# Eight conditioning columns moved out of attention's up projection, and loads of x put between the out projection's weights

## The chip, the cores and the metric

The kernel runs on one core of one Trainium2 chip. The metric is the device time of one execution in microseconds (us). TensorE (PE in the profile) does the matmuls, VectorE (DVE) and ScalarE (ACT) the elementwise work, and SyncE's queue (SP) issues nearly all loads and stores.

## The reference, cut to what matters

One block of a diffusion transformer over 1024 tokens of width 1024. A conditioning vector c gives six column vectors, and the block uses them in this order:

```python
ada = silu(c) @ w_ada + b_ada
sh1, sc1, g1, sh2, sc2, g2 = split(ada, 6)
...
mixed = (g_hy * y_hy + g_att * y_att) @ w_out
x = x + g1 * rmsnorm(mixed, g_mix_post)
hf = rmsnorm(x, g_ffn_pre) * (1 + sc2) + sh2
f = (silu(hf @ w_gate) * (hf @ w_up)) @ w_down
x = x + g2 * rmsnorm(f, g_ffn_post)
```

Here y_att is attention's output times its half of the up weights (attention's up projection), w_out is the out projection, and w_gate, w_up and w_down (width 2816) are the feed-forward part. sc2 is first needed after the out projection, g2 only at the end of the down projection.

## The kernel before, in words

Everything is kept transposed, features on the 128 partitions. Each matmul operand is split into a rounded part ("hi", cast by ACT) and a rest ("lo", subtracted on DVE), and every product is three matmuls: hi by hi, hi by lo, lo by hi. A weight tile is therefore loaded to wraw, cast to whi by ACT (L126) and its wlo is made on DVE (L77 is the helper for all two-tensor operations), before the PE can use it. wraw, whi and wlo have two buffers each.

**A conditioning column** is one column of `cols` (128 numbers). ada_tile (L142 to L146) loads 128 rows of w_ada, 512 KB, into a tile wada_t and multiplies and sums it against silu(c), spread over all partitions, in one DVE instruction on 128x1024 (L145). Columns 0 to 15 (sh1, sc1) are made by matmul at the start, 16 to 31 (g1, sh2) by ada_tile beside attention. The list `jobs` holds columns 32 to 47: sc2 is 32 to 39, g2 is 40 to 47. Tiles wada_t have two buffers here (NWB).

**Attention's up projection** (att_up, L972, called from L983) goes over eight tiles m of the output. Each tile has one weight load of 256 KB (wup), four loads of 256 KB of stored gates (g), 24 matmuls (L134), four sigmoids on ACT, two casts, and on DVE one wlo and eight operations on 128x512: per half the products mix by gate and ps by gate, their sum, and the rest ml. After every two tiles two columns of `jobs` are made (L987 to L989), eight in all: sc2.

**The out projection** (L1128) goes over two halves n of the tokens, two halves z of the output and four pieces q of the weights (wout). A piece is loaded as two halves of 256 KB into one wraw (wide_raw, L1028) and is used for 24 matmuls (rows, L1043). Pieces are counted here from 0 to 15. Two of them are loaded ahead, and wo.next() loads the piece two further on and splits the next. At the head of each half n the eight tiles of x of that half (xh, 256 KB each, L1131) are loaded for the residual. In the half n = 0 one column is made after each piece: columns 40 to 47, g2. A generator `between` turns the result, adds x, makes the second norm and writes x2d; it runs in steps between later matmuls.

**Gate and up** (L1384) goes over products of 12 matmuls each (L1181): for 24 head products and then seven or five products per weight column j (a seven-product scheme for 2x2 blocks). Each product's weights are cast and split (need) one product ahead (LA = 1): the first eight matmuls use whi, the last four wlo. Tiles "xc" have 16 buffers: first x, later results. Tiles "c11" have three, used in the head and at the end. **The down projection** (L1509) is a similar scheme over stored hidden tiles; down_gain needs g2 there (mcol columns 32 to 39).

**What sets the order**: nothing is timed by hand beyond the order of the text. The framework under the kernel orders each engine's instructions by its own estimate of when their inputs and buffers are free, with earlier text first among those that are ready; then each engine and each DMA queue works its list strictly in order. So a load can stand far from where the text has it.

Of the kernel before, what the change touches and what calls it, by code (L numbers as in the profile page):

```python
# [9 lines left out]
F32 = mybir.dt.float32  # L10
F32R = mybir.dt.float32r
I32 = mybir.dt.int32
AF = mybir.ActivationFunctionType
ALU = mybir.AluOpType
# [3 lines left out]
P = 128  # L18

L, D, C, DFF = 1024, 1024, 256, 2816  # L20
KD = D // P
# [8 lines left out]
NWB = 2  # L30
# [28 lines left out]
V_BADA, V_GMPRE, V_GMPOST, V_GFPRE, V_GFPOST = 0, 48, 56, 64, 72  # L59
# [4 lines left out]
def block_kernel(tc, xT, ctxT, cvec, cT, wada1, wada, vecs, lamv, dbias, zT, fw1, fw2, fv, fw3, decay, mfs, mis, rope,  # L64
                 win, wup, wout, wgate, wupf, wdown, outT):
    nc = tc.nc
    V, A, G, T = nc.vector, nc.scalar, nc.gpsimd, nc.tensor
# [8 lines left out]
    def tt(out, a, b, op, eng=None):  # L76
        (eng or V).tensor_tensor(out=out, in0=a, in1=b, op=op)  # L77
# [7 lines left out]
    def act(out, in_, func, bias=0.0, scale=1.0, **k):  # L85
        A.activation(out=out, in_=in_, func=func, bias=bias, scale=scale, **k)
# [14 lines left out]
    cp = root.enter_context(pool("consts", side="left"))  # L101
# [7 lines left out]
    vec = cp.tile([P, NV], F32, name="vec")  # L109
    nc.sync.dma_start(out=vec, in_=vecs)  # L110
    cols = cp.tile([P, 64], F32, name="cols")
    lamc = cp.tile([P, 4], F32, name="lamc")
    mcol = cp.tile([P, 48], F32, name="mcol")
# [28 lines left out]
    def ada_tile(dstcol, sbc, j, tag_pool, nb=NWA):  # L142
        w = tag_pool.tile([P, D], F32, tag="wada", bufs=nb, name="wada_t")
        nc.sync.dma_start(out=w, in_=wada[j - 16])
        V.tensor_tensor_reduce(out=w, in0=w, in1=sbc, scale=1.0, scalar=vec[:, V_BADA + j:V_BADA + j + 1],  # L145
                               op0=ALU.mult, op1=ALU.add, accum_out=dstcol)  # L146
# [510 lines left out]
    for i in range(2):  # L657
        V.tensor_tensor_reduce(out=lamt[:, i * 128:i * 128 + 64], in0=lamt[:, i * 128:i * 128 + 64],
                               in1=lamt[:, i * 128 + 64:i * 128 + 128], scale=1.0, scalar=0.0,
                               op0=ALU.mult, op1=ALU.add, accum_out=lamc[:, i:i + 1])  # L660
# [190 lines left out]
    left = {}  # L851
# [103 lines left out]
    for n in range(2):  # L955
        dg = mp.tile([P, 512], F32, tag="dg", bufs=2, name="dg")
        sl = slice(n * 512, (n + 1) * 512)
# [25 lines left out]
    for m in range(0, 8, 2):  # L983
        ups = [att_up(m), att_up(m + 1)]
        for i in UPO if m == 6 else (0, 0, 1, 1):
            next(ups[i])
        for j in jobs[:2]:  # L987
            ada_tile(cols[:, j:j + 1], sc3, j, left["gp"], NWB)
        jobs = jobs[2:]  # L989
    yst.close()  # L990
    ms_.close()

# [10 lines left out]
    def xc(name):  # L1003
        return rt.tile([P, 512], F32, tag="xc", bufs=16, name=name)
# [89 lines left out]
    def between(n):  # L1094

        sl = slice(n * 512, (n + 1) * 512)
        scale_rows(n, rows_rstd(ssq[:, n], D))
        yield
        acc2 = mp.tile([P, 512], F32, tag="accq", bufs=2, name="accq")

        for k in range(KD):
            z, kq = divmod(k, 4)
            pt = bank2()
            for b in range(4):
                T.transpose(out=pt[:, b * P:(b + 1) * P], in_=om[n, b, z][:, kq * P:(kq + 1) * P], identity=ident)
            stt(xh[n][k], pt, mcol[:, 16 + k:17 + k], xh[n][k], ALU.mult, ALU.add)
            sq_acc(acc2, xh[n][k], k == 0, mp)
            nc.sync.dma_start(out=x2d[:, k, sl], in_=xh[n][k])
        yield
        dg = rstd_dg(pacc, acc2, 512, D, mp, "tr", 2)  # L1110
        yield
        bc = diag_bc(pacc, dg, 512, "tr", 2)
        for k in range(KD):
            stt(xh[n][k], xh[n][k], mcol[:, 24 + k:25 + k], bc, ALU.mult, ALU.mult)
            sh = cols[:, 24 + k:25 + k]
            if n == 0:
                X0[k] = split_tile(rt, "hfa", 16)
                act(X0[k][0], xh[n][k], AF.Identity, bias=sh)
                stt(X0[k][1], xh[n][k], sh, f(X0[k][0]), ALU.add, ALU.subtract)
            else:  # L1120
                act(xh[n][k], xh[n][k], AF.Identity, bias=sh)
        yield
# [4 lines left out]
    wo.split()  # L1127
    for n in range(2):  # L1128
        sl = slice(n * 512, (n + 1) * 512)
        for k in range(KD):  # L1130
            nc.sync.dma_start(out=xh[n][k], in_=xT[k][:, sl])  # L1131
        for z in range(2):
            acc = [bank() for b in range(4)]
            for q in range(4):
                w = wo.next()
                rows(acc, w, [(mixh[k][:, sl], mixl[k][:, sl]) for k in (2 * q, 2 * q + 1)], q == 0, q == 3)
                if n == 1 and 4 * z + q in S0:
                    next(mid)
                if n == 0:
                    for j in jobs[:1]:  # L1140
                        ada_tile(cols[:, j:j + 1], sc3, j, mp, NWB)
                    jobs = jobs[1:]
            for b in range(4):
                sq = mp.tile([P, 512], F32, tag="sqt", bufs=SQB, name="sqt")
                act(sq, acc[b], AF.Square, accum_out=ssq[:, n, b, z:z + 1])
                om[n, b, z] = mp.tile([P, 512], F32, tag="om", bufs=8, name="om")
                A.copy(out=om[n, b, z], in_=acc[b])
        if n == 0:
            mid = between(0)
            tt(mcol[:, 16:24], vec[:, V_GMPOST:V_GMPOST + 8], cols[:, 16:24], ALU.mult)  # L1150
            stt(mcol[:, 24:32], cols[:, 32:40], 1.0, vec[:, V_GFPRE:V_GFPRE + 8], ALU.add, ALU.mult)
        else:
            tt(mcol[:, 32:40], vec[:, V_GFPOST:V_GFPOST + 8], cols[:, 40:48], ALU.mult)
    mx.close()


# [67 lines left out]
    def c11_tile():  # L1224
        return gp.tile([P, 512], F32, tag="c11", bufs=NC11, name="c11")
# [145 lines left out]
    def x_prep(v):  # L1371
        if v < len(xseq):
# [3 lines left out]
            tt(lo, x, f(hi), ALU.subtract)  # L1376
            X[xseq[v]] = hi, lo

    mid = between(1)
    for j in range(2):  # L1380
        src[j] = prep(j, True)
# [2 lines left out]
    for g, (j, p) in enumerate(flat):  # L1384
        if g in S1:
            next(mid)
            if g == S1[3]:
                ws_.close()
                fc = ff.enter_context(pool("ffc", side="left"))
                RA, RB, RC = (rt, "hfa", 16), (gp, "hfb", 16), (fc, "hfc", 24)  # L1390
                mix = combos()
        if g in S2:
            next(mix)
        if g < nhead and p == 2 and j + 2 < NHS:
            src[j + 2] = prep(j + 2, True)
        if g == nhead - LA:
            src[0] = prep(0)
        if g >= nhead and p == 7 and j + 1 < NJ:
            src[j + 1] = prep(j + 1)
        need(g + LA)  # L1400
        head = g < nhead
        if p in (1, 5) or (p == 2 and not head) or (p == 6 and j < NHS):
            b = bank("pj")
        else:
            b = b5[j] if p == 3 else b1[j]
        if j == NF - 1 and p in (7, 2):
            w_load(p == 2)
            if p == 2:
                w_prep(0)
        product(b, wset.pop(g), XT[p], p in (1, 5) or (p == 2 and not head) or (p == 6 and j < NHS))  # L1410
        ring = (lambda: xc("kp")) if j < NHS or j % 2 else p1_tile
        if p == 1:
            b1[j] = b
            p1[j] = evict(p1_tile, b, "p1")
        elif p == 2 and head:
            out_block(j, 0, b, c11_tile)
        elif p == 2:
            tt(p1[j], p1[j], b, ALU.add)
            out_block(j, 0, p1.pop(j))
        elif p == 5:  # L1420
            b5[j] = b
            keep[5] = evict(ring, b, "m5")
        elif p == 6 and j < NHS:
            b1[j] = b
            keep[6] = ring()
            tt(keep[6], p1[j], b, ALU.add)
        elif p == 6:
            keep[6] = evict(ring, b, "e")
        elif p == 3:
            tt(keep[6], keep[6], b, ALU.add)  # L1430
            out_block(j, 1, keep[6])
        elif p == 7:
            if j < NHS:
                f7 = ring()
                tt(f7, p1[j], b, ALU.add)
            else:
                f7 = evict(ring, b, "f")
            tt(keep[5], keep[5], f7, ALU.add)
            out_block(j, 3, keep[5])
        elif j < NHS:  # L1440
            tt(p1[j], p1[j], b, ALU.add)
            out_block(j, 2, p1.pop(j))
        else:
            out_block(j, 2, b, ring)
        if j == NF - 1 and p in (2, 4):
            for v in range(4):
                x_load(4 * (p == 4) + v)
            if p == 2:
                for v in range(4):
                    x_prep(v)  # L1450
# [4 lines left out]

    def down_gain():

        for z in range(2):
            dg = fc.tile([P, 512], F32, tag="s4", bufs=1, name="dg")
            for k in range(4):  # L1460
                ts(dg[:, k * P:(k + 1) * P], ident, mcol[:, 32 + 4 * z + k:33 + 4 * z + k], None, ALU.mult, ALU.bypass)
            A.copy(out=gbc[z], in_=diag_bc(pacc, dg, 512, "tr", 2))
# [206 lines left out]
```

## Time and profile before

| what | us |
|---|---|
| median of three runs (1814.03 to 1820.38) | 1820.0 |
| the profiled execution, whole time | 1822.15 |
| its span, first to last instruction | 1820.3 |
| attention's up projection, first to last matmul | 965.84 to 1021.3 |
| out projection | 1021.32 to 1127.9 |
| gate and up | 1127.92 to 1574.5 |
| down projection and end | 1574.5 to 1820.3 |

The times in the lower rows are counted from the start of the span. In the views a line has the start, the duration, the engine and line, the operation with its tiles (out<-in) and how many such instructions follow one another; in brackets stands the idle time before it and what ended that. In the table by stage each engine has its busy time and its number of instructions. PEclk is the granted TensorE clock: 1.00 is the level of 2.4 GHz, 0.50 that of 1.2 GHz.

### The profile page before, as it was taken

What the parts mean: (1) busy time and instruction counts of PE and PEld (TensorE: products, weight loads), DVE (VectorE), ACT (ScalarE), POOL (GpSimd) and SP (SyncE); (2) the same over time, 40 slices, a digit from 0 to 9 for tenths busy, and PEclk for the clock granted to TensorE, in tenths of its full rate; (3) what the DMA queues carried; (4) which work ended last, traced back from release to release, by engine and by line L of the source; (5) the groups of instructions that cost most, each with busy time, mean ns of one, the idle gap of its engine ahead of it and who ended that gap; (6) DMA issues with size and microseconds to landing.
All of it is one profiled execution on the core that took longest, in us unless ns stands there. A gap on an engine that the chain in (4) does not pass through costs nothing.

```text
span 1820.3 us, 22426 instructions
## 1 busy us (share of the span) xinstructions
PE 1725.2 (95%) x7990; PEld 1380.8 (76%) x7990; DVE 1319.6 (72%) x2357; ACT 769.9 (42%) x1229; POOL 58.2 (3%) x63
## 2 busy tenths in 40 slices
PE   7999989999996999999998799989999999999997
PEld 3588777787875888887876587777778888787785
DVE  4887786867669489898876746777776565767675
ACT  3511323132222376766656356742324333454351
POOL 0000000000001211111000000000000000000000
PEclk9899999999998999999999999999999999999999
DMA  9244533323347744345528663424342333798672
GB/s 333 97 163 161 201 126 122 116 93 134 104 174 277 225 123 142 97 132 192 162 83 304 215 196 125 137 95 151 127 145 87 110 114 112 234 304 260 182 204 71
DMA packets 193615, 292.60 MB, mean 161 GB/s; under 512 B 15155, under 2 KB 115775, under 8 KB 192224
## 3 DMA queue, kind: packets, MB, share of 16 engines
q1 hardware_dynamic: 187280, 283.51, 47.6%
q10 hardware_dynamic: 6224, 7.66, 1.4%
q8 instruction: 63, 1.03, 0.2%
q14 instruction: 48, 0.39, 0.1%
HBM read 215.36 MB, written 75.76 MB: 160 GB/s over the span
## 4 chain that ended last, share of the span: by engine, by line
PE 68%; DVE 19%; DMA 8%; ACT 3%; issue 2%; SPq 0%; ACTq 0%; DVEq 0%
PE pj L1181 19%; PE ps L134 17%; PE ps L1534 8%; DVE pair L77 4%; PE ps L1043 4%; PE S L804 4%; DVE quad L77 3%; PE pt L826 2%; DVE wlo L77 2%; PE psf L392 2%; DMA wraw<-wdown 2%; PE psf L393 2%; PE psf L537 1%; PE pv L835 1%; PE psf L576 1%
## 5 line engine op out<-in xcount | busy, mean ns | idle before, releaser
L77 DVE TENSOR_TENSOR wlo<-wraw,whi 128x512 fp32r<-128x512 f32 (+1 forms) x174 | 158.2, 920 | 161.6 <-ACT whi L126 88.0
L134 PE MATMUL ps<-h_hi,wlo 128*128 128x512 f32 x640 | 174.1, 402 | 0.6 <-DVE wlo L77 0.6
L134 PE MATMUL ps<-h_hi,whi 128*128 128x512 f32 x640 | 173.4, 402 | 0.0
L134 PE MATMUL ps<-h_lo,whi 128*128 128x512 f32 x640 | 167.9, 395 | 0.0
L1534 PE MATMUL ps<-whi,xw 128*128 128x512 f32 x528 | 164.1, 392 | 1.8 <-DVE p L77 0.9
L134 PEld LDWEIGHTS ps<-h_hi,wlo 128*128 128x128 f32 x640 | 119.7, 190 | 24.8 <-DVE wlo L77 1.5
L134 PEld LDWEIGHTS ps<-h_lo,whi 128*128 128x128 f32 x640 | 119.9, 189 | 24.5
L134 PEld LDWEIGHTS ps<-h_hi,whi 128*128 128x128 f32 x640 | 119.6, 191 | 23.0
L1181 PE MATMUL pj<-hfc,whi 128*128 128x512 f32 x528 | 131.8, 392 | 0.2
L1534 PEld LDWEIGHTS ps<-whi,xw 128*128 128x128 f32 x528 | 98.5, 188 | 24.7 <-ACT whi L1023 1.8
L1181 PEld LDWEIGHTS pj<-hfc,whi 128*128 128x128 f32 x528 | 98.5, 188 | 23.2 <-DVE kp L77 2.0
L486 ACT COPY gt<-ps 128x512 f32<-128x512 f32 x56 | 32.9, 588 | 188.7 <-PE ps L134 150.1
L804 PE MATMUL S<-KS,Q 128*128 128x512 f32 (+1 forms) x384 | 108.3, 378 | 2.9 <-DVE pr L808 2.7
L1534 PE MATMUL ps<-wlo,xw 128*128 128x512 f32 x264 | 103.5, 393 | 2.7 <-DVE wlo L77 2.5
L1181 PE MATMUL pj<-hfb,whi 128*128 128x512 f32 x352 | 93.5, 403 | 8.9 <-ACT whi L1173 8.9
L126 ACT CAST whi<-wraw 128x1024 fp32r<-128x1024 f32 (+1 forms) x78 | 74.9, 962 | 51.8 <-PE ps L1043 25.4
L1181 PE MATMUL pj<-hfa,whi 128*128 128x512 f32 x352 | 90.5, 396 | 0.0
L1181 PEld LDWEIGHTS pj<-hfb,whi 128*128 128x128 f32 x352 | 66.9, 191 | 27.4 <-ACT whi L1173 12.0
L1173 ACT CAST whi<-s 128x512 fp32r<-128x512 f32 x66 | 40.5, 621 | 102.0 <-DVE s L77 57.9
L804 PEld LDWEIGHTS S<-KS,Q 128*128 128x128 f32 x384 | 65.5, 191 | 16.9 <-DVE pr L808 8.7
L1181 PEld LDWEIGHTS pj<-hfa,whi 128*128 128x128 f32 x352 | 66.2, 189 | 14.3 <-issue 0.5
L1173 ACT CAST whi<-wraw 128x512 fp32r<-128x512 f32 x88 | 52.2, 618 | 53.6 <-PE pj L1181 44.9
(501 smaller groups left out, 3560.4 us busy)
## 6 DMA issues: line engine op xcount, KB each, us to landing
wraw<-wdown SPq DMA_DIRECT2D x99, 256.0 KB, 4.2
wraw<-win SPq DMA_DIRECT2D x46, 512.0 KB, 4.1
xw<-xd SPq DMA_DIRECT2D x77, 256.0 KB, 5.0
wada_t<-wada SPq DMA_DIRECT2D x32, 512.0 KB, 7.7
wraw<-wgate SPq DMA_DIRECT2D x28, 512.0 KB, 3.5
wraw<-wupf SPq DMA_DIRECT2D x28, 512.0 KB, 3.3
xd<-kp SPq DMA_DIRECT2D x39, 256.0 KB, 2.1
w_ada<-wada SPq DMA_DIRECT2D x16, 512.0 KB, 6.2
```

The source lines that it names most:

```text
L77: (eng or V).tensor_tensor(out=out, in0=a, in1=b, op=op)
L126: A.copy(out=hi, in_=raw)
L134: T.matmul(out=ps, lhsT=w[:, k * P:(k + 1) * P], rhs=xs[k][j], start=start and i == 0, stop=stop and i == len(seq) - 1)
L392: T.matmul(out=out, lhsT=mfm(part, r), rhs=gen[r][:, 0:256], start=True, stop=False)
L393: T.matmul(out=out, lhsT=mfm(pb, rb), rhs=gen[rb][:, 256:512], start=False, stop=True)
L486: A.copy(out=gt, in_=ps)
L804: T.matmul(out=S[:, :cn], lhsT=Q[j][:, i, qt * P:(qt + 1) * P], rhs=KS[i][:, c0:c0 + cn], start=j == 0, stop=j == 1)
L826: T.transpose(out=pt[:, b * 256 + qt * P:b * 256 + (qt + 1) * P], in_=av[qt][:, kt * P:(kt + 1) * P], identity=ident)
L1043: T.matmul(out=acc[b].rearrange("p (m c) -> p m c", m=4), lhsT=xs[kk][i == 1][:, b * P:(b + 1) * P], rhs=w[i == 2][kk], start=first and (k ...
L1173: A.copy(out=hi, in_=src)
L1181: T.matmul(out=ps, lhsT=w[a][:, k * P:(k + 1) * P], rhs=xs[k][b], start=start and i == 0, stop=stop and i == 11, skip_group_check=True)
L1534: T.matmul(out=acc[b], lhsT=X[p, i][xj][:, b * P:(b + 1) * P], rhs=W[p, i][wj], start=p in (5, 1, 3, 2) and (g, q, u) == (0, 0, 0), stop=l ...
```

## The change

Columns 32 to 39 are no longer made in attention's up projection but in the out projection's half n = 0, after pieces 1 to 7, each behind the load of one tile of x; both halves load x in this one-by-one way now. Columns 40 to 47 move into gate and up, from column j = 12 on, one in each j. There each is made in two halves (late_ada): two loads of 256 KB into xc tiles and two DVE instructions on 128x512, with silu(c) loaded and computed once more in two c11 tiles. The product with g_ffn_post moves into down_gain.

```diff
@@ attention's up projection @@
             next(ups[i])
-        for j in jobs[:2]:
-            ada_tile(cols[:, j:j + 1], sc3, j, left["gp"], NWB)
-        jobs = jobs[2:]
@@ out projection @@
         sl = slice(n * 512, (n + 1) * 512)
-        for k in range(KD):
-            nc.sync.dma_start(out=xh[n][k], in_=xT[k][:, sl])
         for z in range(2):
...
                     next(mid)
-                if n == 0:
-                    for j in jobs[:1]:
+                for k in {0: (), 7: (6, 7)}.get(4 * z + q, (4 * z + q - 1,)):
+                    nc.sync.dma_start(out=xh[n][k], in_=xT[k][:, sl])
+                    if n == 0:
+                        j = jobs.pop(0)
                         ada_tile(cols[:, j:j + 1], sc3, j, mp, NWB)
-                    jobs = jobs[1:]
...
-        else:
-            tt(mcol[:, 32:40], vec[:, V_GFPOST:V_GFPOST + 8], cols[:, 40:48], ALU.mult)
@@ gate and up @@
+    ha = cp.tile([P, 48], F32, name="ha")
+    sch = []
+
+    def late_ada(j):
+
+        for z in range(2):
+            sl = slice(z * 512, (z + 1) * 512)
+            if len(sch) == z:
+                sch.append(c11_tile())
+                nc.sync.dma_start(out=sch[z], in_=cvec[:, sl].broadcast_to([P, 512]))
+                act(sch[z], sch[z], AF.Silu)
+            w = xc("wada_h")
+            nc.sync.dma_start(out=w, in_=wada[j - 16][:, sl])
+            V.tensor_tensor_reduce(out=w, in0=w, in1=sch[z], scale=1.0,
+                                   scalar=(ha if z else vec)[:, j if z else V_BADA + j:(j if z else V_BADA + j) + 1],
+                                   op0=ALU.mult, op1=ALU.add, accum_out=(cols if z else ha)[:, j:j + 1])
...
+        if p == 1 and not head and jobs:
+            late_ada(jobs.pop(0))
@@ down_gain @@
+        tt(mcol[:, 32:40], vec[:, V_GFPOST:V_GFPOST + 8], cols[:, 40:48], ALU.mult)
```

## Rows read from the trace of the kernel before

**Rows 1.** The page: span, and TensorE's busy time.
```profile
span 1820.3 us, 22426 instructions
PE 1725.2 (95%) x7990; PEld 1380.8 (76%) x7990; DVE 1319.6 (72%) x2357; ACT 769.9 (42%) x1229; POOL 58.2 (3%) x63
```

**Rows 2.** Busy time by stage: stretch, length, engines with instruction counts, PEclk, DMA.
```profile
965.80:1021.30 55.50, 47.70 (x193) 36.66 (x192) 46.34 (x77) 34.54 (x58) 0.00 (x0) 0.97 0.80 270
...
1203.00:1400.00 197.00, 187.92 (x799) 150.28 (x800) 142.89 (x229) 62.09 (x106) 0.00 (x0) 0.99 0.37 129
1400.00:1574.50 174.50, 174.50 (x762) 142.67 (x761) 102.21 (x167) 69.68 (x121) 0.00 (x0) 1.00 0.34 115
```

**Rows 3.** TensorE in order of time, attention's up projection.
```profile
965.84 1.10 PE L134 MATMUL ps<-y,whi 128*128 128x512 f32 x4
...
974.31 2.89 PE L134 MATMUL ps<-y,whi 128*128 128x512 f32 x8 [2.71 <-ACT whi L126]
...
999.27 1.20 PE L134 MATMUL ps<-y,wlo 128*128 128x512 f32 x4 [1.77 <-DVE wlo L77]
...
1013.75 1.20 PE L134 MATMUL ps<-y,wlo 128*128 128x512 f32 x4 [2.73 <-DVE wlo L77]
```

**Rows 4.** The chain that ended last, around the up projection: start, length, what.
```profile
980.56 1.20 DVE wada_t L145
981.77 0.60 DVE mix L77
```

**Rows 5.** VectorE in order of time, up projection and the first weights behind it.
```profile
970.97 0.69 DVE L77 TENSOR_TENSOR mix<-mix,g 128x512 f32<-128x512 f32 x1 [8.55 <-ACT g L86]
...
998.54 0.68 DVE L77 TENSOR_TENSOR wlo<-wraw,whi 128x512 fp32r<-128x512 f32 x1
...
1013.01 0.69 DVE L77 TENSOR_TENSOR wlo<-wraw,whi 128x512 fp32r<-128x512 f32 x1
...
1027.15 1.21 DVE L77 TENSOR_TENSOR wlo<-wraw,whi 128x1024 fp32r<-128x1024 f32 x1
```

**Rows 6.** TensorE in order of time, start of the out projection.
```profile
1021.32 2.02 PE L1043 MATMUL ps<-whi,mh 128*128 128x512 f32 x8
1023.18 2.03 PE L1043 MATMUL ps<-whi,ml 128*128 128x512 f32 x8
1028.42 2.13 PE L1043 MATMUL ps<-wlo,mh 128*128 128x512 f32 x8 [3.21 <-DVE wlo L77]
...
1041.35 3.78 PE L1043 MATMUL ps<-whi,mh 128*128 128x512 f32 x8 [5.20 <-ACT whi L126]
1044.93 3.00 PE L1043 MATMUL ps<-whi,ml 128*128 128x512 f32 x8
```

**Rows 7.** SyncE's queue in order of time, start of the out projection.
```profile
1028.44 0.37 SPq L1032 DMA_DIRECT2D wraw<-wout  x1
1028.99 4.04 SPq L1131 DMA_DIRECT2D xh<-xT  x8
1034.51 1.69 SPq L1032 DMA_DIRECT2D wraw<-wout  x3
...
1047.02 0.43 SPq L1131 DMA_DIRECT2D xh<-xT  x1
```

**Rows 8.** DMA issues: tile, queue, count, size, median us from issue to landing.
```profile
wraw<-wdown SPq DMA_DIRECT2D x99, 256.0 KB, 4.2
...
wraw<-wout SPq DMA_DIRECT2D x32, 256.0 KB, 4.0
```

**Rows 9.** The column instruction (L145): min, median and max ns.
```profile
L145 DVE CUSTOM_DVE_ANT_0 wada_t<-wada_t,sc,vec x32: 1271/1278/1286, 553.9 to 1064.4; 128x1024 f32<-128x1024 f32 x32
```

**Rows 10.** TensorE in order of time, the first product of gate and up.
```profile
1127.92 1.98 PE L1181 MATMUL pj<-hfa,whi 128*128 128x512 f32 x8
1129.73 1.07 PE L1181 MATMUL pj<-hfa,wlo 128*128 128x512 f32 x4
```

**Rows 11.** Who waited for whom, 960 to 1130 us: total, times, longest.
```profile
DVE wada_t L145 <- DMA wada_t<-wada: 3.2, 4, 2.1
```

## The prediction, made before the changed kernel was run

> **What bounds the kernel now.** The page comes first: TensorE is busy 95% of 1820.3 us [rows 1], so only stretches where it waits can give anything back. The table by stage shows where. From 1400 to 1574.5, in gate and up, it is never idle; in attention's up projection it is busy 47.7 of 55.5 us, and there VectorE is as full as it is, 46.3 us [rows 2]. TensorE in order of time then shows the waits themselves: 2.71 us for a cast (whi) near the start, later 1.77 and 2.73 us for wlo, which VectorE makes [rows 3]; then, in the out projection, 3.21 us for wlo and 5.20 us for whi [rows 6]. These five waits are the stretch that the change touches.
>
> What stands behind each? The chain that ended last runs through VectorE in the up projection, and the columns are links of it at 1.20 us each, twice an ordinary step of 0.60 us [rows 4]. So VectorE, not TensorE, sets the pace there. The 5.20 us have another cause. SyncE's queue issues half of piece 2 at 1028.44, then eight loads of x from 1028.99 on, and the rest of the piece only at 1034.51 [rows 7]; the cast for which TensorE waits cannot start before that has landed. Note also that the order of this queue is not the text's: a load of x for the second half stands at 1047.02, while TensorE is still in the first half. Moving a line moves a load only as far as the framework agrees.
>
> **The change part by part.** *Up projection without columns.* Eight column instructions leave VectorE, 8 x 1.20 = 9.6 us of its chain. What is left per tile is nine steps of 0.60 us, 5.4 us, against 24 matmuls. Eight matmuls take 1.86 us, from 1021.32 to 1023.18 [rows 6], so 24 take 5.6 and the stage's 192 take 44.7 us. VectorE becomes just faster than TensorE. Of the 55.5 us, 10.8 are not matmul pace. The 2.71 us wait and the slow matmuls behind it, eight in 2.89 us [rows 3], stay, since nothing before them changes; the 1.77 and 2.73 us, 4.5 together, can go. Does the new order of VectorE let them go? Keep its old order and strike the columns: wlo of tile 4 stood at 998.54 behind four columns and comes at 993.7; that of tile 6 stood at 1013.01 behind six and comes at 1005.8 [rows 5], done at 1006.5. TensorE, with the early loss of some 5.7 us kept, asks for them at 965.8 + 5.7 + 4 x 5.6 + 0.9 = 994.8 and, two tiles later, 1006.0. So half a microsecond of waiting is left. I take a gain of **4.0 us**; bounds 2.0 (VectorE at 43.2 of 44.7 us has little room) and 5.0.
>
> The loads of these columns go as well, 4 MB of 14 in this stage, and with them their place in SyncE's queue ahead of gates and weights; that only helps, and I count nothing for it.
>
> *First wait of the out projection, 3.21 us.* The wlo of piece 0 is queued on VectorE behind everything of the up projection, at 1027.15 [rows 5]. Without the eight columns it starts 9.6 us earlier and is done at 1018.8. TensorE, starting at 1017.3, first has 16 matmuls that need no wlo, 3.7 us, and asks at 1021.0. The wait goes: **3.2 us**, bounds 0 and 3.2.
>
> *Second wait, 5.20 us.* Behind it the granted clock is at the lower level for a while: the next two groups of eight take 3.78 and 3.00 us where 2.02 is the pace [rows 6], 2.7 us more. Together 7.9. In the new text piece 2 and piece 3 stand ahead of the first load of x. Piece 2's buffer is free when piece 0 is split, at 1018.8; two issues and a landing of 4.0 us at the median [rows 8] bring it to about 1024 to 1025.5, cast and split by 1027.5. TensorE asks for its whi at 1017.3 + 11.2 = 1028.5. It just fits. I take **7.4 us**, bounds 0 (the order of the queue stays) and 7.9.
>
> *What comes in their place in the out projection.* The same 16 loads of x, the same number of columns in the half n = 0 as before. But they now lie between the pieces, and since x has no other wait than its buffers, which are free when mix is done, several of them and two columns may be issued ahead of piece 3. The nearest row for such a wait is the 3.21 us; below it there is nothing, since piece 3 is wanted only 5.6 us after piece 2. I take 0.5 us of loss. On VectorE a column that waits for its load would hold the wlo of the next piece; eight columns are there before and after, so this is no change. The two small products for mcol now wait for the last of sc2's columns, and are needed only at the end of the half n = 1: nothing, covered by some 25 us of matmuls.
>
> *Gate and up.* Sixteen instructions on 128x512 come to VectorE. Half of a column instruction of 1.28 us [rows 9] is 0.64, an ordinary 128x512 step lasts 0.69 [rows 5]: 10.2 to 11.0 us in all. From 1400 to 1574.5 VectorE is idle 72 us and TensorE never; from 1203 to 1400 it is idle 54 us and TensorE waits about 9 [rows 2]. So the time is there. What stands behind such an instruction is the wlo of the next product, which the kernel prepares only one product ahead. The first eight matmuls of a product last 1.81 us before it is needed [rows 10], so one instruction of 0.7 us fits. If the cover is gone, all 11.0 us are on the path. The loads (16 of 256 KB and two of c) go into SyncE's queue beside weights, at a DMA share of 0.34 [rows 2]; a load that waits for an xc tile there would hold a weight load behind it, but there are 16 of them and four results to a pair of columns. ACT gets two more Silus in a stage where it is busy 70 of 174.5 us: nothing. Bounds 0 and 11.0; I take **1.5 us** of loss, nearer to the stretch with no wait at all.
>
> By a rule of the Trainium skill the halving is a loss: "DMA: Bandwidth & Descriptors", Rules for kernel authors, wants loads of 1 MiB and more. No row here shows the same column loaded in both ways. If each extra load cost its fixed 2 us, which that page gives under Anatomy of one DMA (for loads issued by GpSimd), an estimate from the page would be eight times that, 16 us of transfer time, and the sum would be gone if it lay on the path.
>
> **Sum**: 4.0 + 3.2 + 7.4 - 0.5 - 1.5 = **12.6 us** less. The profiled execution took 1822.15 us, 1.85 of them outside its span, and becomes 1809.6; it lies 2.15 above the median of the runs, 1820.0, so against that I say 1807.4.
>
> **The rivals.** *The queue keeps its order.* The framework issues the loads of x as soon as their buffers are free, piece 2 stays behind some of them, and the 7.4 us remain. For it speaks the load at 1047.02, far ahead of its text [rows 7]; against it, that pieces 2 and 3 now stand first in the text. This is also the case in which the change does not do what it says. 4.0 + 3.2 - 2.0 = 5.2 us less: **1814.8**.
>
> *Gate and up has no room.* The framework puts the sixteen instructions not at j = 12 to 19 but where buffers are first free, at the end of the head, where VectorE is full with the operands of the seven products. Then the 11.0 us lie on the path: 14.6 - 0.5 - 11.0 = 3.1 less, **1816.9**. Against it: they have the lowest rank among what is ready.
>
> *Slower: VectorE waits in order for the halves.* Place: gate and up, each half column queued on VectorE right as its load is issued. Price: a 256 KB load of weights lands 4.2 us after issue at the median [rows 8]; the wlo behind it is late by 4.2 - 1.8 = 2.4 us, sixteen times 38.4 us, less the 14.1 gained above: **1844.3**. It makes the kernel slower by over 0.5% from a wait of about 3.3 us per half: (14.1 + 9.1) / 16 = 1.45 us late, and 1.8 of cover. Against it: the earlier columns made VectorE wait four times, 3.2 us together [rows 11]. The skill's rule on small loads, above, points to this rival.
>
> **How the numbers follow.** A measurement here can tell about 0.5%, 9.1 us, from no change. The forecast has a chance of 0.58, the queue's old order 0.17, no room in gate and up 0.13, the slower case 0.12. The first lies below 1810.9 and is faster; the next two lie within 9.1 us of 1820.0: 0.30. All upper bounds, 5.0 + 3.2 + 7.9, give 1803.9, and single runs have lain 6 us below their median, so the range begins at 1800. It reaches over both middle cases to 1821 and leaves out the slower one and strays. The forecast's own range is 1800 to 1811.
>
> **What would show it.** Right: in the up projection no wait for wlo above 1 us; the first wlo of the out projection done before TensorE asks; both halves of piece 2 issued ahead of the first load of x; no wait of 3 us at piece 0, 2 or 3 and a clock of 1.00 through the stage; between 1400 and 1574 still no idle TensorE. Wrong: waits for whi at piece 2 or 3 with loads of x ahead of them; VectorE idle for wada_h in gate and up with a wlo behind; a longer wait of TensorE at the end of the head.

## The result, and the profile after

The changed kernel takes 1799.4 us (median of four runs, 1795.7 to 1802.8) against 1820.0 before (1814.0 to 1820.4): a ratio of 0.9892, interval 0.9874 to 0.9909, and by the medians 20.7 us less (their quotient alone is 0.9887). The profiled execution took 1798.76 us, its span is 1796.8. The forecast was 1807.4. The sign and the case are the forecast's; the gain is 1.6 times as large, and the median lies 0.6 us below the range.

The page, span and TensorE's busy time, to hold against [rows 1]:

```profile
span 1796.8 us, 22465 instructions
PE 1716.9 (96%) x7990; PEld 1376.9 (77%) x7990; DVE 1320.9 (74%) x2373; ACT 769.8 (43%) x1231; POOL 58.1 (3%) x63
```

TensorE has as many instructions as before and is busy 8.3 us less. Of these, 4.6 lie ahead of the up projection, where nothing was changed (below); 3.6 lie in the up and out projections, where matmuls behind a wait had run slowly. VectorE is busy 1.3 us more and the kernel is faster: what changed is where its work stands, not how much it is. The table by stage, in the columns of [rows 2]; the first two rows are the up projection and the out projection, the last two gate and up:

```profile
961.00:1011.00 50.00, 47.32 (x195) 37.41 (x194) 41.02 (x67) 34.32 (x58) 0.00 (x0) 0.97 0.66 216
1011.00:1106.00 95.00, 95.00 (x425) 76.32 (x425) 57.16 (x99) 49.18 (x87) 0.00 (x0) 1.00 0.62 199
...
1181.10:1376.00 194.90, 188.99 (x799) 151.17 (x800) 145.11 (x236) 62.34 (x107) 0.00 (x0) 0.98 0.38 134
1376.00:1550.80 174.80, 174.80 (x762) 142.82 (x761) 110.23 (x190) 69.92 (x121) 0.00 (x0) 1.00 0.40 132
```

The out projection is now full from end to end at a clock of 1.00. Gate and up took the sixteen half columns: over the whole stage VectorE is busy 316.0 us (1106.03 to 1551.03) where it was 305.3 (1127.92 to 1574.76), 110.23 instead of 102.21 us in the last row [rows 2], and TensorE still has no idle time there.

TensorE in order of time, every wait of the stretch and the first uses of wlo and whi behind it, to hold against [rows 3, 6]:

```profile
969.22 3.17 PE L134 MATMUL ps<-y,whi 128*128 128x512 f32 x8 [2.43 <-ACT whi L126]
...
995.80 1.20 PE L134 MATMUL ps<-y,wlo 128*128 128x512 f32 x4 [0.25 <-DVE wlo L77]
...
1006.86 0.62 PE L1040 MATMUL ps<-whi,mh 128*128 128x512 f32 x2
...
1014.33 2.03 PE L1040 MATMUL ps<-wlo,mh 128*128 128x512 f32 x8
...
1021.83 2.03 PE L1040 MATMUL ps<-whi,mh 128*128 128x512 f32 x8
```

Of the five waits named in the prediction, four are gone, and the first, 2.43 us for whi at tile 1, stays as forecast; 0.25 us for wlo at tile 5 are new. The first matmuls of the out projection stand at 1006.86, inside the up projection: their weights are now ready early enough for the framework to mix them in.

SyncE's queue in order of time, to hold against [rows 7]: eight halves of weights, pieces 0 to 3, and behind them the first load of x, as the prediction wanted it.

```profile
1000.02 14.95 SPq L1029 DMA_DIRECT2D wraw<-wout  x8
...
1018.49 0.33 SPq L1135 DMA_DIRECT2D xh<-xT  x1
```

The stretch from the first matmul of the up projection to the first of gate and up took 162.1 us (965.84 to 1127.92) and takes 145.0 (961.01 to 1106.04).

**What is the change's and what is not.** The two spans differ by 23.5 us: 4.8 lie ahead of the up projection, 17.05 in the stretch, 1.8 in gate and up, -0.3 behind it. Up to the up projection the two kernels issue the same instructions on every engine in the same order, so the 4.8 are the spread between executions. So, most likely, are the 1.8: in the runs below the same length is 441.6 to 445.9 us, whether the gate and up stage was changed or not. The change's own worth is the 17 us of the stretch.

### The profile page after: what moved, and what is told of

It is laid out like the page before. It is cut to its first block, busy times and chain, and to the rows that moved or that the text cites. A ratio compares the mean times of both kernels' runs of the same rounds, so it can differ in the third digit from the quotient of the medians.

```text
span 1796.8 us, 22465 instructions
## 1 busy us (share of the span) xinstructions
PE 1716.9 (96%) x7990; PEld 1376.9 (77%) x7990; DVE 1320.9 (74%) x2373; ACT 769.8 (43%) x1231; POOL 58.1 (3%) x63
## 4 chain that ended last, share of the span: by engine, by line
PE 69%; DVE 17%; DMA 8%; issue 2%; ACT 2%; SPq 0%; ACTq 0%; DVEq 0%
PE pj L1175 19%; PE ps L134 18%; PE ps L1548 8%; PE ps L1040 5%; DVE pair L77 4%; PE S L804 4%; DVE quad L77 3%; PE pt L826 2%; PE psf L392 2%; DVE wlo L77 2%; PE psf L393 2%; DMA wraw<-wdown 1%; PE psf L537 1%; PE pv L835 1%; PE psf L576 1%
```

## The experiments

Three sets, each with its own runs of the kernel before (medians 1815.8 us for the four kernels from after_again on, 1815.7 for the four from loads_without_products on, 1817.4 for the last three); ratios are against those. The stretch is the one above, from the profile of each; the next column is from the first matmul of gate and up to the first of the down projection.

| kernel | ratio, interval | up projection begins | stretch | gate and up |
|---|---|---|---|---|
| before | | 965.8 | 162.1 | 446.8 |
| changed | 0.9892, 0.9874 to 0.9909 | 961.0 | 145.0 | 445.0 |
| after_again | 0.9895, 0.9880 to 0.9909 | 962.2 | 143.1 | 441.8 |
| x_one_by_one_only | 0.9947, 0.9932 to 0.9962 | 961.4 | 151.7 | 445.9 |
| columns_only | 0.9888, 0.9875 to 0.9901 | 960.1 | 144.4 | 443.3 |
| no_late_columns | 0.9897, 0.9884 to 0.9910 | 963.8 | 144.5 | 443.2 |
| loads_without_products | 0.9905, 0.9889 to 0.9921 | 962.0 | 145.0 | 443.6 |
| products_without_loads | 0.9978, 0.9965 to 0.9991 | 960.4 | 162.1 | 442.2 |
| silu_after_up | 0.9894, 0.9876 to 0.9911 | 960.1 | 143.9 | 443.8 |
| late_four_times | 0.9887, 0.9871 to 0.9902 | 963.7 | 143.3 | 441.6 |
| eight_per_half | 0.9909, 0.9891 to 0.9928 | 966.2 | 146.1 | 443.9 |
| sixteen_in_first_half | 0.9918, 0.9894 to 0.9942 | 965.3 | 147.2 | 445.1 |
| weights_early | 0.9880, 0.9858 to 0.9902 | 960.3 | 142.8 | 443.7 |

### The changed kernel once more

No edit.

> The changed kernel once more. Both theories: a ratio of 0.987 to 0.991. Its stretch from the first matmul of the up projection to the first of gate and up should again be 145.0 us against 162.1 us before; what the two profiles differ by ahead of that stretch (4.8 us) should not come back, since the instruction lists are the same up to there.

The ratio came back (0.9895). Against a kernel before of 1815.8 us it is worth 19.1 us; the 20.7 of the first set hold a kernel before that ran 4 us longer than in the later sets.

### One part alone: the loads of x

```diff
# against the kernel before
-        for k in range(KD):
-            nc.sync.dma_start(out=xh[n][k], in_=xT[k][:, sl])
...
+                for k in {0: (), 7: (6, 7)}.get(4 * z + q, (4 * z + q - 1,)):
+                    nc.sync.dma_start(out=xh[n][k], in_=xT[k][:, sl])
```

> The kernel before with the loads of x put one by one behind the pieces, and all columns where they were. Theory (the order of SyncE's queue makes the wait at piece 2, VectorE makes the others): the 5.20 us wait and the 2.7 us of slow clock go, the waits of 1.77, 2.73 and 3.21 us for wlo stay; the stretch takes 154 to 155 us, the ratio is about 0.996. Rival (VectorE's backlog sets when the pieces' buffers come free, so order alone does little): 160 to 162 us, ratio 0.999 to 1.000.

10.4 us of the stretch went, ratio 0.9947. The waits for wlo stay: 1.75, 1.89 and 2.73 us, where they were 1.77, 2.73 and 3.21 [rows 3, 6]. None follows at piece 2. That is worth the 7.9 us of wait and slow matmuls that were expected. Most of the other 2.5 us lie where this edit has no part: the twelve matmuls behind the wait at tile 1 take 2.9 us here and 4.4 before. TensorE in order of time:

```profile
1007.42 1.20 PE L134 MATMUL ps<-y,wlo 128*128 128x512 f32 x4 [1.89 <-DVE wlo L77]
...
1021.60 2.13 PE L1043 MATMUL ps<-wlo,mh 128*128 128x512 f32 x8 [2.73 <-DVE wlo L77]
```

SyncE's queue in order of time shows why no wait follows; compare [rows 7]. Pieces 2 and 3 are issued together, four halves, before the first load of x:

```profile
1021.62 2.65 SPq L1032 DMA_DIRECT2D wraw<-wout  x4
1024.32 0.98 SPq L1138 DMA_DIRECT2D xh<-xT  x2
```

### The other part alone: the columns

```diff
# against the changed kernel
+        for k in range(KD):
+            nc.sync.dma_start(out=xh[n][k], in_=xT[k][:, sl])
         for z in range(2):
...
-                    nc.sync.dma_start(out=xh[n][k], in_=xT[k][:, sl])
```

> The changed kernel with the eight loads of x of each half put back at its head; all columns as in the changed kernel. Theory: the waits for wlo go, a wait of about 5 us with its slow clock comes back at piece 2; the stretch takes 152 to 154 us, the ratio is about 0.995. Rival (with VectorE free the pieces are split so early that x does no harm): 145 to 146 us, ratio as the changed kernel's, 0.989.

The rival that was named held and the theory fell: the whole gain is here as well (0.9888, stretch 144.4), with x at the head of the half as before. There is no wait in the out projection: the last one before gate and up is that of tile 4 of the up projection.

```profile
987.29 1.20 PE L134 MATMUL ps<-y,wlo 128*128 128x512 f32 x4 [0.83 <-DVE wlo L77]
```

Its SyncE queue in order of time: eight halves of weights, pieces 0 to 3, from 998.54 on, and only then the eight loads of x.

```profile
998.54 14.94 SPq L1029 DMA_DIRECT2D wraw<-wout  x8
1013.82 0.81 SPq L144 DMA_DIRECT2D wada_t<-wada  x2
1017.00 3.65 SPq L1128 DMA_DIRECT2D xh<-xT  x8
```

Its VectorE in order of time: the wlo of pieces 0, 1 and 2, then the last ml.

```profile
1008.98 1.22 DVE L77 TENSOR_TENSOR wlo<-wraw,whi 128x1024 fp32r<-128x1024 f32 x1
...
1011.32 1.22 DVE L77 TENSOR_TENSOR wlo<-wraw,whi 128x1024 fp32r<-128x1024 f32 x1
...
1015.14 1.23 DVE L77 TENSOR_TENSOR wlo<-wraw,whi 128x1024 fp32r<-128x1024 f32 x1 [1.40 <-ACT whi L126]
1016.28 0.68 DVE L77 TENSOR_TENSOR ml<-mix,mh 128x512 fp32r<-128x512 f32 x1
```

Piece 0 is split at 1010.2 and its buffer is then free for piece 2. The first load of x stands at 1017.00, right behind the end of the last ml at 1016.96, which is what it waited for in the trace: x takes its buffers when mix is done. In the kernel before, the wlo of piece 0 ended at 1028.36 [rows 5] and the last ml, from 1028.29 on for 0.68 us, at 1028.97; x followed at 1028.99 [rows 7]. There the buffers of x and of piece 2 became free almost together, and in the framework's order the eight loads of x came between the two halves of piece 2. With VectorE free early, piece 2's buffer is free some 7 us before those of x, and both halves go first although the text has x first. So the order of the queue is still what brings piece 2 in time, but here VectorE makes that order and not the text.

### Loads or products?

The eight columns of the up projection were two things, 4 MB of loads and 9.6 us of VectorE. Each kernel keeps one of them, at the old place.

```diff
# against the kernel before: loads_without_products
-            ada_tile(cols[:, j:j + 1], sc3, j, left["gp"], NWB)
+            ada_tile(cols[:, j:j + 1], sc3, j, left["gp"], NWB, 8)   # sums 8 of the 1024 numbers
# against the kernel before: products_without_loads
-            ada_tile(cols[:, j:j + 1], sc3, j, left["gp"], NWB)
+            V.tensor_tensor_reduce(out=still, in0=sc3, in1=sc3, scale=1.0, scalar=vec[:, V_BADA + j:V_BADA + j + 1],
+                                   op0=ALU.mult, op1=ALU.add, accum_out=cols[:, j:j + 1])
```

> The kernel before, where the eight columns of the up projection keep their loads of 512 KB but the VectorE instruction covers 8 of the 1024 numbers (sc2 is wrong by the rest that is left out). Theory (VectorE's time was the cost): the waits for wlo in the up projection and at piece 0 go, 1.77 + 2.73 + 3.21 us, the wait at piece 2 stays with its slow clock; stretch 153 to 156 us, ratio 0.995 to 0.997. Rival (the 4 MB and their place in SyncE's queue were the cost): 160 to 162 us, ratio 0.999 to 1.000.

> The kernel before, where the eight columns of the up projection have no loads and VectorE multiplies and sums silu(c) by itself in their place (sc2 is left out and something else stands there). Theory: the waits for wlo stay; stretch 160 to 162 us, ratio 0.998 to 1.000. Rival (loads and queue): 153 to 156 us, ratio 0.995 to 0.997.

With the loads and without the products the stretch is 145.0 us, as in the changed kernel; two other waits for wlo stand in its up projection, 1.09 us at tile 2 and 0.72 at tile 7. With the products and without the loads it is 162.1, as before, with the three waits for wlo and the one at piece 2 in their old places. TensorE in order of time, the kernel without the loads:

```profile
1007.16 1.86 PE L134 MATMUL ps<-y,wlo 128*128 128x512 f32 x4 [1.77 <-DVE wlo L77]
...
1022.87 2.13 PE L1045 MATMUL ps<-wlo,mh 128*128 128x512 f32 x8 [2.71 <-DVE wlo L77]
...
1035.97 3.78 PE L1045 MATMUL ps<-whi,mh 128*128 128x512 f32 x8 [5.37 <-ACT whi L126]
```

and the kernel without the products, the only wait of its out projection:

```profile
1028.29 0.73 PE L1043 MATMUL ps<-whi,mh 128*128 128x512 f32 x2 [0.22 <-ACT whi L126]
```

In its queue, seven halves of weights go ahead of x, which has its old place in the text:

```profile
999.51 15.73 SPq L1032 DMA_DIRECT2D wraw<-wout  x7
1015.52 0.34 SPq L144 DMA_DIRECT2D wada_t<-wada  x1
1016.86 3.67 SPq L1131 DMA_DIRECT2D xh<-xT  x8
```

So VectorE's time stands behind all four waits. The expectation had left the one at piece 2 to the queue: 153 to 156 us were forecast for the kernel without the products. The 4 MB cost nothing in the stretch, at a DMA share of 0.80 [rows 2]. The ratio of the kernel without loads, 0.9978, is still a little under 1 though its stretch is that of before; where those 4 us lie was not found, and a single profile of each kernel can't tell it from the spread.

### Do the late columns cost anything?

```diff
# against the changed kernel: no_late_columns
-        if p == 1 and not head and jobs:
-            late_ada(jobs.pop(0))
+    V.memset(cols[:, 40:48], 1.0)
# against the changed kernel: late_four_times
+            for i in range(3):
+                V.tensor_tensor_reduce(out=w, in0=w, in1=sch[z], scale=1.0, scalar=vec[:, V_BADA + j:V_BADA + j + 1],
+                                       op0=ALU.mult, op1=ALU.add, accum_out=ha[:, 8 + i:9 + i])
```

> The changed kernel without columns 40 to 47: g2 is left out and set to one. Theory: they cost about 1.5 us, gate and up takes 443 to 445 us against 444.8, ratio at most 0.001 below the changed kernel's. Rival (VectorE has no room in gate and up): 5 to 11 us faster than the changed kernel.

> The changed kernel with each late half product done four times over (48 instructions more on VectorE, some 36 us; g2 is wrong, the repeated product standing in its place). Theory: VectorE has 65 us of idle time in that part of gate and up, most of it takes them, but some wlo are now late: 2 to 15 us more than the changed kernel. Rival (VectorE is near its limit there, each instruction is paid): 30 us more or over.

Nothing that can be measured here: 0.9897 without them, 0.9895 with them, 0.9887 with four times the products, each with an interval of some 0.0015, 2.5 us, to either side. In gate and up VectorE is busy 304.9, 316.5 and 347.2 us in the three. In the changed kernel's trace the tile wada_h (min, median and max ns; the second half is alike) and VectorE's waits in gate and up and in the out projection:

```profile
L1386 DVE CUSTOM_DVE_ANT_0 wada_h<-wada_h,c,vec x8: 745/747/753, 1361.7 to 1482.9; 128x512 f32<-128x512 f32 x8
```

```profile
DVE wada_h L1386 <- DMA wada_h<-wada: 3.4, 3, 1.8
...
DVE wada_t L145 <- DMA wada_t<-wada: 14.7, 7, 3.0
```

VectorE does wait in order for loads, as the slower rival said: 3.4 us for halves, and in the out projection 14.7 us for columns, where it was 3.2 [rows 11]. TensorE waits for none of it.

### Was the late place needed?

Two kernels make g2 in the out projection too and have no late columns: one column per piece in both halves, or two per piece in the first.

```diff
# against the changed kernel, both
-        if p == 1 and not head and jobs:
-            late_ada(jobs.pop(0))
# eight_per_half
-                    if n == 0:
-                        j = jobs.pop(0)
-                        ada_tile(cols[:, j:j + 1], sc3, j, mp, NWB)
+                    j = jobs.pop(0)
+                    ada_tile(cols[:, j:j + 1], sc3, j, mp, NWB)
# sixteen_in_first_half
-                        j = jobs.pop(0)
-                        ada_tile(cols[:, j:j + 1], sc3, j, mp, NWB)
+                        for i in range(2):
+                            j = jobs.pop(0)
+                            ada_tile(cols[:, j:j + 1], sc3, j, mp, NWB)
```

> The changed kernel without its late columns: the eight of g2 are made in the half n = 1 of the out projection, one per piece, as sc2's are in the half n = 0 (all 16 columns are computed, none in gate and up). Theory (VectorE's time in the up projection was the cost, and both halves of the out projection have room: VectorE 57 of 95 us, DMA share 0.62): the stretch from the first matmul of the up projection to the first of gate and up stays at 143 to 145 us, TensorE waits nowhere in the out projection for over 1 us, the ratio is 0.988 to 0.991, as with the late columns. Rival (the half n = 1 has no room, since VectorE also turns the first half's result and adds x there): waits of TensorE for wlo in the half n = 1, 3 us and more in all, a stretch of 147 us or longer, a ratio of 0.991 to 0.994.

> All 16 columns in the half n = 0 of the out projection, two per piece, none in gate and up. Loads in that half: 8 pieces of 512 KB, 8 tiles of x of 256 KB and 16 columns of 512 KB, 14.7 million bytes in some 47.5 us, 309 GB/s; the up projection of the kernel before moved 270 GB/s at a DMA share of 0.80, so the share would be about 0.92. Theory (the DMA queue now sets the pace there): waits of TensorE for whi, 2 to 6 us in all, a stretch of 147 to 151 us, a ratio of 0.991 to 0.993. Rival (transfers stay hidden, as all else in this stretch once VectorE has time): a stretch of 143 to 146 us and a ratio of 0.988 to 0.991.

Neither has a wait for weights in the out projection. What grows is TensorE's waits at the transposes of the result (L1102): 3.0 and 3.7 us in all, against 1.7 in the changed kernel. The table by stage of the second kernel, half n = 0 and half n = 1:

```profile
1011.00:1058.50 47.50, 47.50 (x205) 38.18 (x203) 31.51 (x44) 16.90 (x30) 0.00 (x0) 1.00 0.87 272
1058.50:1112.50 54.00, 52.00 (x240) 41.20 (x239) 39.22 (x79) 32.58 (x59) 0.00 (x0) 1.00 0.62 200
```

The share of 0.92 that was expected was not reached, since the columns did not stay in the first half: with two buffers for wada_t the last load was issued at 1065.1. The ratios, 0.9909 and 0.9918, are above 0.9895 by 2.5 and 4 us (by the medians 4 and 6), but the intervals overlap: the late place is worth a few microseconds at most, and these runs don't settle whether it is worth any.

### The wait that is left

```diff
# against the changed kernel: silu_after_up (Silu of c behind the up projection, its load unmoved)
-    silu_bc(sc3)
+    nc.sync.dma_start(out=sc3, in_=cvec.broadcast_to([P, D]))
...
+    sc4 = mp.tile([P, D], F32, name="sc4")
+    act(sc4, sc3, AF.Silu)
# against the changed kernel: weights_early (weights of tiles 0 and 1 ahead of tile 0's gates)
-        ups = [att_up(m), att_up(m + 1)]
+        ups = [att_up(i, wload(wup[i][:, 512:1024], 4) if m == 0 else None) for i in (m, m + 1)]
```

> The changed kernel with the Silu of c, which no longer has a user in the up projection, moved behind it (into a tile whose memory comes free at the end of the up projection). Theory: on ScalarE the Silu and its table load, 2.4 us, stand ahead of the sigmoids and of whi for tile 1, and make the one wait left in the up projection, 2.43 us, with about 1.7 us of slow clock behind it; both go: stretch 141 us against 145, ratio about 0.002 below the changed kernel's. Rival (the gates' loads set that wait): no change, or a loss of up to 3 us where the first column in the out projection now waits for the Silu and holds a wlo.

> The changed kernel with the weights of the up projection's tiles 0 and 1 loaded ahead of the stored gates of tile 0, aimed at the wait of 2.43 us for whi at tile 1, the longest that is left. Theory (the weights are late because they stand behind the gates in SyncE's queue): the wait at tile 1 falls below 0.5 us and nothing takes its place, 2.4 us of 1799 less, a ratio of about 0.988. Rival (as when the load and Silu of c were moved: the queue is full here, and the next load is late instead): a wait of 1 to 3 us at tile 2 or for the gates' results, the ratio unchanged at 0.989 to 0.990.

Without the Silu the wait at tile 1 went, and one for whi came at tile 3. With the weights first it went too, and three smaller ones came at tiles 3, 4 and 5. TensorE in order of time, first silu_after_up, then weights_early:

```profile
975.16 0.51 PE L134 MATMUL ps<-y,whi 128*128 128x512 f32 x1 [1.85 <-ACT whi L126]
```

```profile
974.35 1.21 PE L134 MATMUL ps<-y,whi 128*128 128x512 f32 x4 [0.81 <-ACT whi L126]
...
980.67 1.20 PE L134 MATMUL ps<-y,whi 128*128 128x512 f32 x4 [0.44 <-ACT whi L126]
993.79 1.20 PE L134 MATMUL ps<-y,wlo 128*128 128x512 f32 x4 [0.48 <-DVE wlo L77]
```

What changed at tile 1 is ScalarE's order. The weights of tile 1 were issued at 949.92 in the changed kernel, at 949.22 and 949.64 in these two, some 10 us ahead of the first gates in all three; so the theory of weights_early, weights late behind the gates, does not hold for them. But in the changed kernel their cast stood on ScalarE behind the Silu and four sigmoids, two of which waited for their gates. In these two it stands ahead of the sigmoids. ScalarE in order of time, that cast in the changed kernel, in silu_after_up and in weights_early:

```profile
968.57 0.60 ACT L126 CAST whi<-wraw 128x512 fp32r<-128x512 f32 x1
960.75 0.62 ACT L126 CAST whi<-wraw 128x512 fp32r<-128x512 f32 x1
963.37 0.60 ACT L126 CAST whi<-wraw 128x512 fp32r<-128x512 f32 x1
```

weights_early has the shortest stretch, 142.8 us, and the lowest ratio, 0.9880, but its interval holds the changed kernel's 0.9892. None of these kernels is shown to beat the changed one.

## Why the prediction was right, and where it was off

**The case.** VectorE set the pace of the up projection, and the products of its eight columns were the cause: right, and shown by the pair that splits loads from products. The 4 MB of loads, counted at nothing, are nothing in that stretch. Where the prediction went wrong is the reason for its largest term, the second wait, and some sizes.

**The sum against the stretch.** Forecast for the stretch: 4.0 + 3.2 + 7.4 - 0.5 = 14.1; measured 17.05. TensorE's idle time there falls from 16.2 to 2.7 us, 13.5, and its busy time by 3.6. The 2.95 more come from the four terms below, 0.25 + 0.8 + 0.5 + 0.5, and from 0.9 us of matmul time that was traced to no single wait.

- *Up projection*, 4.0: the waits for wlo fall from 4.50 to 0.25 us, 4.25. The forecast of half a microsecond left was good. The waits for whi in tiles 1 and 3, 3.26 us together, are 2.43; counted at no change, this is 0.8 more.
- *First wait*, 3.2: gone. The framework even put piece 0's wlo ahead of the last mix steps, at 1010.46.
- *Second wait*, 7.4: 5.20 us of idle time are gone and with them the 2.7 of slow matmuls, 7.9. The size was about right; **the reason was not**, and so the size is in part luck. The step said that piece 2 comes in time because the loads of x now stand behind it in the text. The new text suffices for that, as x_one_by_one_only shows, but it isn't needed: columns_only has x at the head and no wait, since VectorE frees piece 2's buffer before those of x. And the two can't be added. Alone they take 10.4 and 17.7 us off the stretch, together 17.1 (19.0 in the second profile): beside the columns' move, the loads of x one by one bring nothing that these runs show.
- *New wait in the out projection*, -0.5: there is none.

This bears on the first rival too, the queue's old order. With x first in the text, as that order would want it, piece 2 still went ahead, and the 7.9 us went. No kernel with VectorE free early held piece 2 behind x, so what that would cost, the rival's 1814.8, stays untested.

**The mis-sized term outside.** The 1.5 us of loss in gate and up are not seen, though they lie within the 2.5 us that these intervals leave open. VectorE's share was counted well: a half takes 0.75 us and 0.08 to read the sum out, but the next instruction starts 0.67 us after it (1361.71 to 1362.38), and over the stage VectorE is busy 10.7 us more, inside the 10.2 to 11.0 of the prediction. What was missing is how much room there is: the stage takes four times that work without a loss that can be measured. The rule of the Trainium skill for large loads ("DMA: Bandwidth & Descriptors", Rules for kernel authors: 128 partitions and 1 MiB or more per DMA for the most bandwidth) is not borne out here as a loss of time, in a stage where the DMA engines are busy 0.38 to 0.40: with all sixteen loads gone the ratio is 0.9897 against 0.9895. Whether a column lands later in two halves is not shown: of each kind the trace has only two landings, 4.0 us both times for a half, 8.7 and 5.9 for a whole column, in other stages.

**The rest.** 20.65 measured against 12.6 is 8.05 more. The stretch gives 2.95 of it, gate and up 3.3 (1.5 not lost, 1.8 between executions). The remaining 1.8 is spread too: 4.8 ahead of the stage, less 0.3 behind it and less the 2.7 by which the difference of the two profiled executions, 23.4, exceeds that of the medians. By the later sets the gain is about 19 us, which the range, reaching down to 1800, would have just held.

**What the rivals got.** No room in gate and up: fell with late_four_times, whose gate and up takes 441.6 us with four times the work. VectorE waiting in order for halves: the mechanism is there, 3 of 16 times and 1.8 us at the longest, but the operand behind it is not late for TensorE.

## What to carry to other kernels

Price small work by what is full where it stands: 9.6 us of VectorE cost 17 us in a stage where VectorE sets the pace, and 11 us of it cost nothing that could be measured where it has gaps. When a wait for a load is found, ask which engine frees the buffer before blaming the queue's order: a late split by VectorE let the loads of x in ahead of piece 2 here, and either an earlier split or another text put it right. Where two edits each remove the same wait, their gains don't add, and only a kernel with each alone shows which one is needed.

## What had not been expected of the hardware

- In the half n = 0 of the changed kernel the DMA engines are busy 0.87 of 47 us and move 277 GB/s, and TensorE waits for no load. VectorE's 14.7 us of waiting for columns is where the pressure shows.
- The wait left at tile 1 is followed by matmuls of different pace: eight took 3.17 us after 2.43 us of idle time, 2.89 after 2.71 [rows 3], but 2.12 after 2.50 in x_one_by_one_only. The granted clock just behind the wait is 0.68 (969.2 to 974.6) in the changed kernel, 0.66 (974 to 979) before, and 1.00 (969.6 to 974.0) in x_one_by_one_only. In silu_after_up it falls behind a wait of only 1.85 us (0.66 from 975 to 980). So the length of the wait alone does not tell whether the clock falls; what else does stays open.
- The up projection begins anywhere from 960.1 to 966.2 us (table), in kernels that differ only behind that point or, in three of them, by little ahead of it (one small instruction in no_late_columns, the order around tile 0 in silu_after_up and weights_early). A difference of two profiles holds up to 6 us that a change further on has no part in; the stretch alone is cleaner.
